# A hybrid attention / RWKV-7 / GLA layer on one core: the order on each engine, taken from a list schedule inside the kernel

## The chip, the cores and the metric

The kernel runs on one core of one Trainium2 chip. The metric is the device time of one execution in microseconds (us). The kernel before was timed three times: 2271.08, 2274.56 and 2274.71 us, with a median of 2274.56 us. One more execution was profiled, and all rows of the profile come from that one.

A core has several engines, each of which works through its own instructions strictly in order: PE multiplies matrices, DVE and ACT and POOL work on elements, and SP issues transfers (DMA). An instruction that waits for another engine holds up all that stands behind it on its own engine. So the order on each engine is part of the program.

## The reference

The input is x with 4096 tokens of width 1024. One layer is computed. An RMS norm that a conditioning vector scales and shifts gives h. One projection of h feeds three groups of heads: attention over a sliding window of 128 tokens, RWKV-7 time mixing, and GLA, a linear attention with a forget gate. Each group is multiplied by its own SiLU gate. One output projection, a norm and a gated addition close the layer:

```python
h = _rmsnorm(x, g_pre) * (1.0 + scale[:, None]) + shift[:, None]
proj = h @ w_in
...
attn = _sliding_window_attention(aq, ak, av, sinks) * jax.nn.silu(ag)
...
def step(S, inp):                       # RWKV-7, once for each token
    r_t, w_t, k_t, v_t, kk_t, a_t = inp
    sa = jnp.einsum('bhvk,bhk->bhv', S, -kk_t)
    S = (S * w_t[:, :, None, :] + sa[..., None] * (kk_t * a_t)[:, :, None, :]
         + v_t[..., None] * k_t[:, :, None, :])
    return S, jnp.einsum('bhvk,bhk->bhv', S, r_t)
...
rwkv = _rwkv7_mixer(...) * jax.nn.silu(rg)
gla = _gla_mixer(...) * jax.nn.silu(gg)
y = jnp.concatenate([attn, rwkv, gla], axis=-1) @ w_out
return x + gate[:, None] * _rmsnorm(y, g_post)
```

All is in float32.

## The kernel before

The tokens are cut into 16 tiles of 256. To keep float32 accuracy, every projection is done with numbers split in two float16 halves (names ending in h and l), and takes three matmuls for each block of 128 input columns: high by high, high by low, low by high.

**Stage 1** begins with a prologue: the conditioning vector is worked out (matmuls adp and gp on sums acc that DVE or POOL make), and weights are loaded and split. Then each tile passes these streams: "a" normalises x and transposes it to hT; "p" projects; "w" makes decays and GLA gates; "qa", "qb" and "qc" make the matrices of the RWKV chunks and solve their triangular systems (Xp, Xs, Xq, D, td); "q2" is the recurrence over the four chunks of 64 tokens in a tile; "r", "v" and "k" make GLA, its values (pv) and the keys (kp, yt, ot on the way); "c" prepares the weights of stage 2 in pieces (cs, ch, cl). Stage 1 writes hT and the mixed results to DRAM.

One chunk of the recurrence is a chain across engines. PE makes rp, from the chunk's own matrices and from the state Sst; DVE copies it to rs; PE makes up; ACT copies it to UV; PE makes sp; DVE adds and scales it (Ss) to the next state. The next chunk's rp needs that state.

**Stage 2** does attention and the output. Between the two stages stand the load of further weights, the first tile's projections and a branch to a fallback. Then each tile runs: "p2" (projection q, k, v: matmuls qp, kp, vp; gates gp; the output projection of the tile before: op), "s" (scores sc, softmax pr, ovp) and "m". Stream m multiplies by the gates (mx), sums its squares on ACT, adds them over partitions by one small matmul mp, makes a power of two msc from it on DVE (mtot, p2e, p2f, msc), and with it splits mx into the two halves of mT: the high one on ACT, the low one on DVE. The output projection op reads mT:

```python
S.activation(mT[:, 0].rearrange("p k n -> p (k n)"), mx.rearrange("p k n -> p (k n)"), AF.Square, accum_out=mss)
yield [mss, "mq"]
mp = mq("mp")
PE.matmul(mp[:, 0:1], ones, mss, start=True, stop=True)
...
pow2(msc, miv, mtot)
...
yield [msc]
for g in range(2):
    S.activation(mT[:, 0, ks], mx[:, ks], AF.Identity, scale=msc)
    V.scalar_tensor_tensor(mT[:, 1, ks]..., mx[:, ks]..., msc, mT[:, 0, ks]..., op0=ALU.mult, op1=ALU.subtract)
```

**What sets the order.** Each stream is a Python generator; a `yield` names the tiles or the PSUM banks that it needs next. `emit` picks, again and again, the stream that a coarse model of times says can go on first, and among equals the one of the lowest rank; what that stream issues until its next `yield` goes into the program. The model's costs are in `LANES` and `HOP`, and each operation passes through `Lane.__getattr__`, a helper whose line (72) therefore stands at every row of the profile. The framework's own scheduler then orders the instructions of each engine, with the program's order as their priority and costs of its own. Nothing in the kernel fixes its result.

## Time and profile before

| what | value |
|---|---|
| median of three runs | 2274.56 us |
| the profiled execution's own time | 2265.72 us |
| its span, from the first instruction to the last | 2263.9 us |
| mean granted clock of PE | 0.985 |
| PE busy | 91% |
| DVE, ACT, POOL busy | 66%, 49%, 9% |
| distance between the output projections of two tiles in stage 2 | about 66 us |

Stage 1 ends near 1060 us and the tiles of stage 2 run from about 1290 to 2220 us. The waits of PE are read as "tile that PE waited to make, what ended the wait: us in total, number of waits, longest". On the timeline a row is "start, length, engine, line, operation, output<-inputs, how many", and in brackets the idle time of the engine before it and what ended that. In a row by windows the columns are the window, its length, the busy times of PE, weight load, DVE, ACT and POOL with their instructions, the granted clock of PE, the busy share of the DMA engines and the GB/s that they moved.

## The change

The kernel now keeps a second record of every operation. `Order.note` is called from the helper (now line 299) and stores the engine, how long the operation holds it, after how long its result can be used, and which earlier operations it must follow: by overlapping regions of tiles, by PSUM banks, and by the reuse of buffers, for which the pools are wrapped to tell their number of buffers. `Order.pin` then runs a list schedule over the record. It takes the engine that can start earliest, and on it, of the operations that are ready by then, the one that comes first in the program. PE's model knows that a change of the array's shape waits until the array is empty; ACT's knows the load of a table; SP's knows a time for a transfer by its size. Last, each operation is tied to the one that the schedule put ahead of it on its engine, by a dependency without a semaphore, so that the framework's scheduler has no choice left.

This is done twice: for all of stage 1, and for the streams of stage 2. What stands between, from the load of stage 2's weights to the fallback, is not tied. The operations themselves, their tiles and buffers stay as they were.
